# A two-layer hybrid block on one core: scale vectors as columns, squares summed by TensorE, an opening in fixed issue order, condition rows kept in DRAM

## The chip, the core and the metric

The program runs on one core of a Trainium2 chip. A core has five engines that work beside each other: TensorE (PE) for matmuls, VectorE (DVE), ScalarE (ACT), GpSimd (POOL), and SyncE (SP), which here issues the DMAs. The metric is the device time of one execution in microseconds, lower being better; shown is the median of the runs. PE weight loads appear as an engine of their own in the profile, PEld.

## What is computed

Two layers (`DEPTH` 2, `D_MODEL` 1024) over 512 latent tokens `x` and 256 context tokens `ctx`. A conditioning vector gives shift, scale and gate for the tokens, another one the same for the context. Each layer normalizes, projects once, runs four token mixers (latent attention, windowed attention, axial attention, a gated recurrence), gates and merges them, and adds the result. All is float32. The change touches only how the modulation and the normalization of layer 0 are made, and where the condition rows come from later:

```python
def _rms_norm(x, gain):
    y = x32 * lax.rsqrt(jnp.mean(x32 * x32, axis=-1, keepdims=True) + RMS_EPS)
    return (y * gain)
def _layer(x, ctx, mod_x, mod_c, lp, rope, update_ctx):
    shift_x, scale_x, gate_x = jnp.split(mod_x[:, None, :], 3, axis=-1)
    shift_c, scale_c, gate_c = jnp.split(mod_c, 3, axis=-1)
    hx = _rms_norm(x, lp['norm_w']) * (1 + scale_x) + shift_x
    hc = _rms_norm(ctx, lp['norm_w']) * (1 + scale_c) + shift_c
    px = _project_stream(hx, lp, rope, True)
    pc = _project_stream(hc, lp, None, update_ctx)
...
    sc = jax.nn.silu(c)
    scc = jax.nn.silu(c_ctx)
...
        mod_x = sc @ w_mod[l] + b_mod[l]
        mod_c = scc @ w_mod[l] + b_mod[l]
        x, ctx = _layer(x, ctx, mod_x, mod_c, lp, rope, l < DEPTH - 1)
```

## The kernel before

The streams are kept transposed: `x` and `ctx` stand as eight tiles `xk[k]` of 128 channels by 768 tokens (512 of `x`, 256 of the context). float32 matmuls of the projections are split in three: a value is kept as a rounded high half and a low half (`hi`, `lo`), and `mm3` multiplies hi·hi, lo·hi and hi·lo. So every weight tile is loaded by a DMA into `wraw`, rounded by ACT (`whi`) and subtracted by POOL (`wlo`), and every activation `hx[k]` needs its high half from ACT and its low half from a subtraction. Other matmuls, with plain float32 operands, appear as two records each.

The opening, which is what the change is about, has these steps, each with the name it has in the rows:

- `cond` (L246 and after, matmuls `scb` at L252, copies at L254): the two condition vectors, spread over all 128 partitions as rows `sc[0]` and `sc[1]` of 1024, which lie in the ring `P`. Each is made from eight matmuls 128x128 and two ACT copies. It is called for the opening, again in layer 0 in the recurrence stage, and for one row in layer 1, since attention uses `P` in between.
- `sumsq` (L286 to L290): ACT squares a tile, DVE adds it to the sum; `rstd_cols` (L299) sums over partitions on PE with two columns of ones, DVE adds epsilon (`xms`, L302) and POOL raises to the power -1/2 (L304); `rstd_rows` (L310) spreads the result as `rb`.
- `scale_pe` (L227 to L238): the scale of two channel tiles, with the two condition columns `scol` as the stationary operand and the weights moving 256 columns at a time; the result, two rows, is copied by ACT and turned into columns by two matmuls (L232), then DVE makes `mod` and `s1` (shown as `s`).
- `shift0` (L243): a shift is a DVE product-and-sum over a weight tile and a condition row, for the tokens and for the context.
- `normal` (L929): `xk` times `rb` on DVE. `hx_split` (L331 to L333): ACT writes the high half and the full value, DVE subtracts.
- `first`: the first column groups of the projection, matmuls `tk`. They accumulate tile by tile, so PE can start on `hx[0]` before `hx[1]` is there. Behind them follow matmuls `tg`, for which all eight tiles are needed, and then the head norms (`hn_ss`) and the attention.

The opening's weights come in four chunks `c`, each with two scale tiles `wmp{c}_0/1`, two shift tiles `wmp{c}_2/3` and two weight tiles for `first`. The program is written in this order, but a scheduler of the language, which works from its own timeline, sets the order of each engine's instructions; `issue_after` pins single ones. SP issues the DMAs of its queue in order, and waits there for buffers to come free.

Of the kernel before, what the change touches and what calls it, by code (L numbers as in the profile page):

```python
# [59 lines left out]
NS = len(SLOT)  # L60


def body(tc, xT, ccol, wmod, wmod0, pvec, rvec, tabs, wall, out):
# [5 lines left out]
    with st:  # L69
# [64 lines left out]
        xs = dp.tile([4, 128, 2, SEQ], F32, name="xs")  # L134

# [12 lines left out]
        def vectors():  # L148
# [72 lines left out]
        def scale_pe(c, scol, ws, p, pm):  # L221

            for q in range(2):
                w = ws[q]
                for e in range(4):
                    k = 4 * q + e
                    pe.matmul(out=p[0:2, :256], lhsT=scol[:, 2 * k:2 * k + 2], rhs=w[:, e * 256:e * 256 + 256],  # L227
                              start=(k == 0), stop=(k == 7))
            r = raw_take()
            act.activation(out=r[0:2, :256], in_=p[0:2, :256], func=AF.Copy)  # L230
            for e in range(2):
                last = pe.matmul(out=pm[:, 2 * e:2 * e + 2], lhsT=r[0:2, e * 128:e * 128 + 128], rhs=ident[0:2, 0:2],  # L232
                          start=True, stop=True, skip_group_check=True)
            f = 8 + 2 * c
            col = lambda o: pv[:, o:o + 2].unsqueeze(2).to_broadcast([128, 2, 2])
            dve.tensor_tensor(out=mod[0][:, f:f + 2, :], in0=pm[:, 0:4].rearrange("p (f i) -> p f i", f=2),
# [3 lines left out]
            return last  # L240
# [53 lines left out]

        def rstd_cols(state, n, p):
            T = n // 128
            acc = state['acc']
            for t in range(T):
                state['ins'] = pe.matmul(out=p[:, 2 * t:2 * t + 2], lhsT=acc[:, t * 128:t * 128 + 128], rhs=ones2,  # L299
                          start=True, stop=True, skip_group_check=True)  # L300
# [25 lines left out]
        def hx_split(k, i, h, xk):  # L326
# [6 lines left out]
            dve.tensor_tensor(out=h[:, 1, sl], in0=xk[:, sl], in1=h[:, 0, sl].bitcast(F32), op=ALU.subtract)  # L333
# [558 lines left out]
        scol = silu_col()  # L892
        xt = [big(f"x{kp}") for kp in range(4)]
# [4 lines left out]
        for kp in range(4):  # L898
            sp.dma_start(out=xt[kp][:, :, SEQ:], in_=xT[kp][:, :, SEQ:])
        xk = [xt[k // 2][:, k % 2, :] for k in range(KT)]  # L900
        sc = [cond(scol, i, crow[i]) for i in range(2)]
        states = [{}, {}]
        for k in range(KT):
            sumsq(xk[k][:, :SEQ], k, states[0])
# [30 lines left out]
        ms = rstd_cols(states[0], SEQ, mp[:, 384:])  # L935
        last = [scale_pe(0, scol, wm[0], mp, mp[:, 256:])]
        rstd_rows(ms, SEQ, rb)
        for c in range(4):
            for g in w0:
                w0[g].append(wload0((g, c)))  # L940
            if c < 3:
                wm.append(mod0_load(c + 1))
                with tc.issue_after(last[0].ins):
                    last[0] = scale_pe(c + 1, scol, wm[c + 1], mp, mp[:, 256:])
            ks = (2 * c, 2 * c + 1)
            for k in ks:
                shift(0, k)
            if c == 0:
                for k in range(KT):
                    normal(0, k)  # L950
            for k in ks:
                hx_split(k, 0, hx[k], xk[k])
                shift(1, k)
            for k in ks:
                first(k, (0, 2))
            if c == 0:
                for k in range(KT):
                    sumsq(xk[k][:, SEQ:], k, states[1], rawt[:, 1024:1280])
                with tc.issue_after(last[0].ins):
                    ms = rstd_cols(states[1], CTX, mp[:, 384:])  # L960
                last[0] = states[1]['ins']
                rstd_rows(ms, CTX, rb)
            for k in ks if c else ():
                normal(1, k - 2)
                hx_split(k - 2, 1, hx[k - 2], xk[k - 2])
                first(k - 2, (4,))
# [227 lines left out]
```

## Time and profile before

| | us |
|---|---|
| median of 3 runs | 1434.54 |
| lowest, highest | 1434.51, 1438.37 |
| profiled execution | 1437.18 |
| its span in the trace (2.1 lie around it) | 1435.1 |
| PE busy | 1357.7 (95%) |
| DVE, ACT, POOL busy | 895.2, 675.9, 712.3 |

Times in the rows are counted from the start of the span. A row of the timeline gives start and length of one instruction or of several alike (x4), the engine, the source line, the operation and its tiles, output before the arrow; in brackets stands how long the engine had been idle, and what ended that. Because matmuls overlap in the array, the distance of two starts is the better measure of what one costs than its own length. Lines are those of the kernel before; helpers give the same line for many tiles.

### The profile page before, as it was taken

The numbers are of one execution on the slowest core, as the hardware profiler recorded it, in microseconds if no ns is written. First come the engines' busy times: TensorE is split into PE (matmuls) and PEld (weight loads), VectorE is DVE, ScalarE is ACT, GpSimd is POOL, SyncE is SP. The second block draws the span as 40 slices with busy tenths as digits, with TensorE's granted clock in tenths as the row PEclk, the third lists the DMA queues.
The fourth block names the chain that finished last, engine by engine and source line by source line (L and its number), as shares of the span: only waits on it lengthen the run. The fifth ranks groups of instructions, "written<-read, shape, count | busy, mean of one in ns | idle before, by whom it ended". The sixth has DMA issues, their size and how long they took to land.

```text
span 1435.1 us, 21997 instructions
## 1 busy us (share of the span) xinstructions
PE 1357.7 (95%) x8216; PEld 1189.2 (83%) x8216; DVE 895.2 (62%) x1473; ACT 675.9 (47%) x1413; POOL 712.3 (50%) x691
## 2 busy tenths in 40 slices
PE   6898999999999999999999889999999999898998
PEld 4697989999998897888888778998887777776786
DVE  7756876456747656677445777876577576466441
ACT  4544555445544444562232344655555454465331
POOL 1453614223624625577553466455345563478663
PEclk8899999999999999999999999999999999999999
DMA  9301101111111212322335732112221111222544
GB/s 353 92 5 59 34 16 55 42 45 39 54 37 38 59 30 81 103 65 98 125 114 158 234 95 75 45 48 74 67 61 45 61 57 39 59 67 66 188 153 144
DMA packets 58746, 117.81 MB, mean 82 GB/s; under 512 B 6544, under 2 KB 10640, under 8 KB 58640
## 3 DMA queue, kind: packets, MB, share of 16 engines
q1 hardware_dynamic: 58640, 116.42, 25.7%
q8 instruction: 64, 1.05, 0.3%
q14 instruction: 42, 0.34, 0.1%
HBM read 112.20 MB, written 4.19 MB: 81 GB/s over the span
## 4 chain that ended last, share of the span: by engine, by line
PE 72%; DVE 9%; POOL 7%; DMA 5%; issue 4%; ACT 3%; SPq 0%; POOLq 0%; ACTq 0%; DVEq 0%
PE fg L196 9%; PE fg L195 9%; PE fg L197 9%; PE pvo L567 4%; DMA wraw<-in_wall_dram 3%; PE tg L197 3%; PE tg L196 3%; PE tg L195 3%; PE s L587 3%; POOL wlo L190 3%; PE pj L195 2%; PE pj L196 2%; PE pj L197 2%; PE ptr L560 2%; PE ptr L561 2%
## 5 line engine op out<-in xcount | busy, mean ns | idle before, releaser
L190 POOL TENSOR_TENSOR wlo<-wraw,whi 128x512 fp32r<-128x512 f32 (+2 forms) x290 | 398.8, 1378 | 360.9 <-ACT whi L189 347.3
L196 PE MATMUL fg<-hx,wlo 128*128 128x512 f32 (+1 forms) x864 | 314.2, 364 | 12.3 <-POOL wlo L190 12.3
L195 PE MATMUL fg<-hx,whi 128*128 128x512 f32 (+1 forms) x864 | 313.9, 365 | 7.9 <-ACT whi L189 5.0
L197 PE MATMUL fg<-hx,whi 128*128 128x512 f32 (+1 forms) x864 | 312.0, 361 | 0.0
L189 ACT ACTIVATE whi<-wraw 128x512 fp32r<-128x512 f32 (+2 forms) x290 | 179.8, 621 | 229.2 <-DMA wraw<-in_wall_dram 154.4
L196 PEld LDWEIGHTS fg<-hx,wlo 128*128 128x128 f32 x864 | 166.4, 193 | 38.9 <-POOL wlo L190 16.3
L195 PEld LDWEIGHTS fg<-hx,whi 128*128 128x128 f32 x864 | 165.6, 192 | 33.8 <-ACT whi L189 7.1
L197 PEld LDWEIGHTS fg<-hx,whi 128*128 128x128 f32 x864 | 166.1, 192 | 22.2
L564 DVE TENSOR_TENSOR PT<-ptr,PT 128x512 fp32r<-128x512 f32 (+1 forms) x148 | 98.5, 672 | 60.6 <-ACT PT L563 59.3
L196 PE MATMUL tg<-whi,hx 128*128 128x256 f32 (+1 forms) x432 | 122.5, 285 | 1.9 <-DVE hx L323 1.9
L195 PE MATMUL tg<-whi,hx 128*128 128x256 f32 (+1 forms) x432 | 122.2, 285 | 1.8 <-ACT hx L322 1.2
L197 PE MATMUL tg<-wlo,hx 128*128 128x256 f32 (+1 forms) x432 | 121.5, 284 | 1.4 <-POOL wlo L190 1.4
L563 ACT ACTIVATE PT<-ptr 128x512 fp32r<-128x512 f32 (+1 forms) x148 | 84.7, 585 | 79.6 <-PE ptr L561 70.0
L537 ACT ACTIVATE P<-s,nm 128x768 f32<-128x768 f32 (+3 forms) x120 | 91.9, 771 | 55.7 <-DVE nm L532 30.1
L530 DVE TENSOR_REDUCE nm<-s 128x2 f32<-128x1536 f32 (+3 forms) x60 | 86.0, 1434 | 29.5 <-PE s L197 16.9
L865 POOL TENSOR_TENSOR acc<-acc,gt 128x768 f32<-128x768 f32 (+1 forms) x48 | 81.1, 1690 | 24.1 <-DVE gt L861 23.2
L196 PEld LDWEIGHTS tg<-whi,hx 128*128 128x128 f32 x432 | 82.6, 191 | 2.8 <-DVE hx L323 2.5
L195 PEld LDWEIGHTS tg<-whi,hx 128*128 128x128 f32 x432 | 82.5, 191 | 2.8 <-ACT hx L322 1.4
L197 PEld LDWEIGHTS tg<-wlo,hx 128*128 128x128 f32 x432 | 82.4, 191 | 2.2 <-POOL wlo L190 2.0
L853 ACT ACTIVATE gt<-fg 128x512 f32<-128x512 f32 x84 | 44.1, 525 | 74.5 <-PE fg L197 70.9
L551 DVE TENSOR_SCALAR P<-P,den 128x768 f32<-128x768 f32 (+3 forms) x120 | 77.4, 685 | 1.8
L560 PE MATMUL ptr<-ident,P 128*128 128x128 f32 x288 | 72.9, 279 | 1.9 <-DVE gt L861 1.8
(302 smaller groups left out, 3137.2 us busy)
## 6 DMA issues: line engine op xcount, KB each, us to landing
wraw<-in_wall_dram SPq DMA_DIRECT2D x286, 256.0 KB, 2.6
raw<-in_wmod_dram SPq DMA_DIRECT2D x32, 512.0 KB, 3.6
wmp<-in_wmod_dram SPq DMA_DIRECT2D x16, 512.0 KB, 8.6
x<-in_xT_dram SPq DMA_DIRECT2D x4, 512.0 KB, 5.7
xs<-xn SPq DMA_DIRECT2D x4, 512.0 KB, 3.9
gt<-xs SPq DMA_DIRECT2D x8, 256.0 KB, 2.9
out_dram<-xn SPq DMA_DIRECT2D x4, 512.0 KB, 3.8
wraw<-in_wall_dram SPq DMA_DIRECT2D x8, 160.0 KB, 2.2
```

The lines of the kernel that those rows point to most:

```text
L189: act.activation(out=hi[:, :n], in_=raw, func=AF.Copy)
L190: pool.tensor_tensor(out=lo[:, :n], in0=raw, in1=hi[:, :n].bitcast(F32), op=ALU.subtract)
L195: pe.matmul(out=o, lhsT=a[0], rhs=b[0], start=first, stop=False, skip_group_check=True)
L196: pe.matmul(out=o, lhsT=a[1], rhs=b[0], start=False, stop=False, skip_group_check=True)
L197: pe.matmul(out=o, lhsT=a[0], rhs=b[1], start=False, stop=last, skip_group_check=True)
L530: dve.tensor_reduce(out=nm, in_=s3, axis=AX.X, op=ALU.max, negate=True)
L537: act.activation(out=P[i][:, :L], in_=s3[:, i, :], func=AF.Exp, scale=scale, bias=nm[:, i:i + 1], accum_out=den[:, i:i + 1])
L551: dve.tensor_scalar(out=P[i][:, :L], in0=P[i][:, :L], scalar1=den[:, i:i + 1], scalar2=None, op0=ALU.mult)
L560: pe.transpose(tr[:, e * 256:e * 256 + 128], P[0][:, ca:ca + 128], ident)
L563: act.activation(out=q[:, :n], in_=tr[:, :n], func=AF.Copy)
L564: dve.tensor_tensor(out=q[:, 512:512 + n], in0=tr[:, :n], in1=q[:, :n].bitcast(F32), op=ALU.subtract)
L865: pool.tensor_tensor(out=a[:, :N], in0=a[:, :N], in1=t[:, :N], op=ALU.add)
```

## The change

`scale_pe` takes the weights as stationary operand, 128x128 at a time, and moves the two condition columns over them, so the scale comes out as columns, without the copy and the two transposes; its DVE part becomes `scale_add`. `sumsq_pe` takes the place of `sumsq` in the opening (the later norms keep `sumsq`'s form): the square of each tile goes to PE, which sums it with the columns of ones for every 128 tokens and adds up over the eight tiles in PSUM. `hx_split` leaves the context's low half to POOL. A class `InOrder` wraps PE, ACT and DVE for the opening: each instruction is pinned behind the one before on its engine, so these three follow the written order, which is rewritten. The small vectors of the recurrence (`vectors`) are pinned on DVE behind the opening. A DRAM tile `cs` takes the two condition rows after the opening, and layers 0 and 1 read it in place of calling `cond`.

```diff
+class InOrder:
+    def __init__(self, tc, eng, last=None):
+        self.tc, self.eng, self.last = tc, eng, last
+    def __getattr__(self, name):
+        f = getattr(self.eng, name)
+        def call(*a, **k):
+            if self.last is None:
+                self.last = f(*a, **k)
+            else:
+                with self.tc.issue_after(self.last.ins):
+                    self.last = f(*a, **k)
+            return self.last
+        return call
...
+        cs = dp.tile([2, 128, 1024], F32, name="cs")
...
-        def scale_pe(c, scol, ws, p, pm):
-            for q in range(2):
-                w = ws[q]
-                for e in range(4):
-                    k = 4 * q + e
-                    pe.matmul(out=p[0:2, :256], lhsT=scol[:, 2 * k:2 * k + 2], rhs=w[:, e * 256:e * 256 + 256],
-                              start=(k == 0), stop=(k == 7))
-            r = raw_take()
-            act.activation(out=r[0:2, :256], in_=p[0:2, :256], func=AF.Copy)
-            for e in range(2):
-                last = pe.matmul(out=pm[:, 2 * e:2 * e + 2], lhsT=r[0:2, e * 128:e * 128 + 128], rhs=ident[0:2, 0:2],
-                          start=True, stop=True, skip_group_check=True)
+        def scale_pe(c, scol, ws, p):
+            for k in range(KT):
+                w = ws[k // 4]
+                for e in range(2):
+                    a = (k % 4) * 256 + e * 128
+                    pe.matmul(out=p[:, 2 * e:2 * e + 2], lhsT=w[:, a:a + 128], rhs=scol[:, 2 * k:2 * k + 2],
+                              start=(k == 0 and e == 0), stop=(k == KT - 1), skip_group_check=True)
...
+        def sumsq_pe(xk, k, sq, p):
+            n = xk.shape[1]
+            act.activation(out=sq[:, :n], in_=xk, func=AF.Square)
+            for t in range(n // 128):
+                pe.matmul(out=p[:, 2 * t:2 * t + 2], lhsT=sq[:, t * 128:t * 128 + 128], rhs=ones2,
+                          start=(k == 0 and t == 0), stop=(k == KT - 1), skip_group_check=True)
...
-            dve.tensor_tensor(out=h[:, 1, sl], in0=xk[:, sl], in1=h[:, 0, sl].bitcast(F32), op=ALU.subtract)
+            (pool if i else dve).tensor_tensor(out=h[:, 1, sl], in0=xk[:, sl], in1=h[:, 0, sl].bitcast(F32), op=ALU.subtract)
...
+        pe, act, dve = (InOrder(tc, e) for e in (nc.tensor, nc.scalar, nc.vector))
...
+        for k in range(KT):
+            sumsq_pe(xk[k][:, :SEQ], k, gt_take(), rb)
+        scale_pe(0, scol, wm[0], mp[:, 0:4])
+        ms = rstd_cols(None, SEQ, rb)
+        scale_add(0, mp[:, 0:4])
         rstd_rows(ms, SEQ, rb)
...
             ks = (2 * c, 2 * c + 1)
+            if c == 0:
+                for k in ks:
+                    normal(0, k)
             for k in ks:
                 shift(0, k)
+                hx_split(k, 0, hx[k], xk[k])
+            first(ks[0], (0, 2))
+            q = mp[:, 4 * c + 4:4 * c + 8]
+            if c < 3:
+                scale_pe(c + 1, scol, wm[c + 1], q)
+            first(ks[1], (0, 2))
             if c == 0:
+                for k in range(2, KT):
+                    normal(0, k)
+            if c < 3:
+                scale_add(c + 1, q)
+            if c == 1:
                 for k in range(KT):
...
+                    sumsq_pe(xk[k][:, SEQ:], k, gt_take(), rb)
+                rstd_rows(rstd_cols(None, CTX, rb), CTX, rb)
+                for k in range(4):
+                    shift(1, k)
+                for k in range(KT):
+                    normal(1, k)
+            if c == 2:
+                for k in ks:
+                    shift(1, k)
+                for k in (0, 1):
+                    context(k)
         for k in (6, 7):
...
+            shift(1, k)
+        for k in range(2, KT):
+            context(k)
+        boot = dve.last
+        pe, act, dve = nc.tensor, nc.scalar, nc.vector
         consts()
+        for i in range(2):
+            sp.dma_start(out=cs[i], in_=sc[i])
...
-                sc = [cond(scol, i, crow[i]) for i in range(2)]
+                for i in range(2):
+                    sp.dma_start(out=sc[i], in_=cs[i])
...
-                sc = [cond(scol, 0, crow[0])]
+                sp.dma_start(out=sc[0], in_=cs[0])
```

On PE, from the start to the first `tk`, the kernel before has this order (`ones_92` are the columns of ones, `scol` the condition columns, `P` in the second row the sum of squares):

```order
L252 MATMUL scb<-ident,scol 128x128 x16
L299 MATMUL mp<-ones_92,P 128x2 x4
L227 MATMUL mp<-wmp_0_123,scol 2x256 x4
L227 MATMUL mp<-wmp_1_124,scol 2x256 x4
L310 MATMUL rb<-ident,xms 128x128 x4
L232 MATMUL mp<-ident,raw 128x2 x2
```

In the changed kernel all rows of the opening have a line of `InOrder`, and PE has there:

```order
L73 MATMUL scb<-ident,scol 128x128
L76 MATMUL scb<-ident,scol 128x128 x15
L76 MATMUL rb<-ones_92,gt 128x2 x32
L76 MATMUL mp<-scol,wmp_0_124 128x2 x8
L76 MATMUL mp<-scol,wmp_1_125 128x2 x8
L76 MATMUL rb<-ident,xms 128x128 x4
```

The four sums over partitions have become 32, the eight scale matmuls 16 with two columns, and the transposes are gone.

On DVE, between the normals of the tokens and the low halves of tiles 0 to 3, before has among others this piece (`ISA raw,mod_99` with the row under it is one shift):

```order
L236 TENSOR_TENSOR mod_99<-mp,consts 128x4
L333 TENSOR_TENSOR hx_0_175<-x_115,hx_0_175 128x512
L333 TENSOR_TENSOR hx_1_176<-x_115,hx_1_176 128x512
L243 ISA raw,mod_99<-wmp_3_351,P,consts 128x1024
L243 ISA mod_99 128x1
L243 ISA wmp_2_350,mod_99<-wmp_2_350,P,consts 128x1024
L243 ISA mod_99 128x1
L290 TENSOR_TENSOR raw<-raw,gt 128x256
```

For the same two tiles the changed kernel has:

```order
L76 ISA raw,mod_99<-wmp_2_126,P,consts 128x1024
L76 ISA mod_99 128x1
L76 TENSOR_TENSOR hx_0_157<-x_116,hx_0_157 128x512
L76 ISA raw,mod_99<-wmp_3_127,P,consts 128x1024
L76 ISA mod_99 128x1
L76 TENSOR_TENSOR hx_1_158<-x_116,hx_1_158 128x512
```

A shift now stands directly ahead of the low half of its own tile, where before the shifts of a chunk stood well ahead of its low halves, with other chunks' shifts and adds between.

On SP, around the layer-0 recurrence, the two reloads of the condition rows (into `P`) stand behind the recurrence's own weights and ahead of the next weight tiles:

```order
L795 DMA wraw<-in_wall_dram 128x512 x2
L1086 DMA P<-cs 128x1024 x2
L208 DMA wraw<-in_wall_dram 128x512 x3
L281 DMA raw<-in_wmod_dram 128x1024
L208 DMA wraw<-in_wall_dram 128x512 x2
```

Before, there was no DMA between the first two rows on `wraw`. Outside the opening and the two recurrence stages the order of all engines is nearly the same in both kernels.

## Rows read from the trace of the kernel before

**Rows 1.** Timeline of the opening to 22 us: start, us, engine, line, operation [idle].

```profile
3.31 6.69 PE L252 MATMUL scb<-ident,scol 128*128 128x128 f32 x32 [3.31 <-DVE scol L209]
...
9.99 3.08 DVE L290 TENSOR_TENSOR P<-P,gt 128x512 f32<-128x512 f32 x4 [1.01 <-ACT gt L289]
...
10.86 1.14 ACT L289 ACTIVATE gt<-x 128x512 f32<-128x512 f32 x2
11.91 0.58 ACT L254 ACTIVATE P<-scb 128x512 f32<-128x512 f32 x1
...
13.13 1.87 PE L299 MATMUL mp<-ones,P 128*128 128x2 f32 x8 [3.13 <-DVE P L290]
...
15.28 2.06 POOL L304 TENSOR_TENSOR xms<-xms,mhalf 128x4 f32<-128x4 f32 x1 [14.00 <-DVE xms L302]
...
20.93 1.16 PE L310 MATMUL rb<-ident,xms 128*128 128x128 f32 x8
```

**Rows 2.** Timeline, 22 to 59 us: normals, scale, shift, `hx` and the first `tk`.

```profile
22.70 3.07 DVE L929 TENSOR_TENSOR x<-x,rb 128x512 f32<-128x512 f32 x5
...
25.90 5.30 PE L227 MATMUL mp<-wmp,scol 128*2 128x256 f32 x16 [3.29 <-DVE mod L236]
...
29.16 1.28 DVE L243 CUSTOM_DVE_ANT_0 raw<-wmp,P,consts 128x1024 bf16<-128x1024 f32 x1
...
31.52 1.50 ACT L332 ACTIVATE x<-x,mod,s 128x512 f32<-128x512 f32 x2
...
34.73 1.29 DVE L333 TENSOR_TENSOR hx<-x,hx 128x512 fp32r<-128x512 f32 x2
...
35.47 0.39 PE L196 MATMUL tk<-w,hx 128*128 128x256 f32 x1 [3.07 <-DVE hx L333]
...
56.00 2.73 DVE L929 TENSOR_TENSOR x<-x,rb 128x256 f32<-128x256 f32 x8
```

**Rows 3.** Timeline, DVE and POOL from 42 us.

```profile
42.41 4.00 POOL L190 TENSOR_TENSOR w<-wraw,w 128x512 fp32r<-128x512 f32 x2 [17.69 <-ACT w L189]
...
42.97 2.30 DVE L243 CUSTOM_DVE_ANT_0 wmp<-wmp,P,consts 128x1024 f32<-128x1024 f32 x1
```

**Rows 4.** Timeline, end of the opening: last low halves, first `tg`, end of `tg`.

```profile
77.19 2.12 DVE L333 TENSOR_TENSOR hx<-x,hx 128x512 fp32r<-128x512 f32 x4 [3.36 <-ACT x L332]
...
88.80 0.28 PE L195 MATMUL tg<-whi,hx 128*128 128x256 f32 x1
...
106.08 0.39 PE L195 MATMUL fg<-hx,whi 128*128 128x512 f32 x1
```

**Rows 5.** Instructions of line 299: records, ns min/median/max, first and last start.

```profile
L299 PEld LDWEIGHTS mp<-ones,P x8: 288/334/338, 13.1 to 14.6; 128*128 128x128 f32 x8
...
L299 PE MATMUL ssp<-ones,P x8: 165/252/252, 827.1 to 827.8; 128*128 128x2 f32 x8
```

**Rows 6.** Busy us by stretch: length, PE, PEld, DVE, ACT, POOL, clock, DMA, GB/s.

```profile
13.00:14.00 1.00, 0.87 (x4) 0.87 (x5) 0.08 (x1) 0.00 (x0) 0.00 (x0) 0.50 1.04 400
20.00:21.00 1.00, 1.00 (x6) 0.30 (x4) 1.00 (x3) 0.12 (x1) 0.80 (x1) 1.00 1.00 393
20.00:30.00 10.00, 6.71 (x29) 3.04 (x28) 9.89 (x18) 2.90 (x7) 3.05 (x2) 0.83 1.04 398
100.00:110.00 10.00, 8.45 (x63) 7.80 (x62) 7.02 (x19) 3.87 (x11) 9.25 (x13) 1.00 0.09 26
110.00:120.00 10.00, 8.01 (x52) 6.77 (x50) 7.64 (x13) 3.74 (x9) 7.08 (x8) 1.00 0.27 80
120.00:130.00 10.00, 8.34 (x34) 6.67 (x35) 6.64 (x14) 4.79 (x13) 2.05 (x2) 0.83 0.16 52
```

**Rows 7.** Chain that ended last, in the two recurrence stages: start, us, what.

```profile
548.99 0.89 PE scb L252 x8
...
556.95 2.76 DMA wraw<-in_wall_dram
...
1327.14 2.70 DMA wraw<-in_wall_dram
```

More of the change, by code (lines that the diff above doesn't have):

```diff
@@ L146, in consts, with vectors @@
             dve.tensor_copy(out=maskb, in_=mask)
-        def vectors():
+        def vectors(last):
+            dve = InOrder(tc, nc.vector, last)
             ab = tp.tile([128, 8], F32, name="sp_ab", tag="sm")
@@ L239, in scale_pe @@
                                      in1=col(PV_NORM + 2 * c), op0=ALU.add, op1=ALU.mult)
-            return last
         def shift0(f, i, sc, w, out):
@@ L293, in rstd_bcast @@
             return rstd_rows(rstd_cols(state, n, tps("ssp")), n, tps("rb"))
+        def sumsq_pe(xk, k, sq, p):
[4 more added lines that the diff above has]
+                          start=(k == 0 and t == 0), stop=(k == KT - 1), skip_group_check=True)
         def rstd_cols(state, n, p):
             T = n // 128
-            acc = state['acc']
-            for t in range(T):
-                state['ins'] = pe.matmul(out=p[:, 2 * t:2 * t + 2], lhsT=acc[:, t * 128:t * 128 + 128], rhs=ones2,
+            for t in range(T) if state else ():
+                pe.matmul(out=p[:, 2 * t:2 * t + 2], lhsT=state['acc'][:, t * 128:t * 128 + 128], rhs=ones2,
                           start=True, stop=True, skip_group_check=True)
@@ L933, in shift, with context @@
             shift0(k, i, sc[i], w, w if i else rawt[:, 1536:2048].bitcast(BF16))
-        ms = rstd_cols(states[0], SEQ, mp[:, 384:])
-        last = [scale_pe(0, scol, wm[0], mp, mp[:, 256:])]
+        def context(k):
+            hx_split(k, 1, hx[k], xk[k])
+            first(k, (4,))
+        for k in range(KT):
[3 more added lines that the diff above has]
+        scale_add(0, mp[:, 0:4])
         rstd_rows(ms, SEQ, rb)
@@ L940, in body @@
                 w0[g].append(wload0((g, c)))
+            if c == 1:
+                for kp in range(4):
+                    sp.dma_start(out=xt[kp][:, :, SEQ:], in_=xT[kp][:, :, SEQ:])
             if c < 3:
                 wm.append(mod0_load(c + 1))
-                with tc.issue_after(last[0].ins):
-                    last[0] = scale_pe(c + 1, scol, wm[c + 1], mp, mp[:, 256:])
             ks = (2 * c, 2 * c + 1)
+            if c == 0:
+                for k in ks:
+                    normal(0, k)
@@ L946, in body @@
             for k in ks:
                 shift(0, k)
-            if c == 0:
-                for k in range(KT):
[L950 to L956, printed above, removed]
-                for k in range(KT):
[L958 to L966, printed above, removed]
-        for k in (6, 7):
-            normal(1, k)
-            hx_split(k, 1, hx[k], xk[k])
-            first(k, (4,))
+                hx_split(k, 0, hx[k], xk[k])
[4 more added lines that the diff above has]
+            first(ks[1], (0, 2))
@@ L1024, in body @@
             if l == 0:
-                with tc.issue_after(wdma[0].ins):
-                    vectors()
+                vectors(boot)
             m1 = branch(SWA)
```

9 lines of the change are left out of this document (3 added, 6 removed).

## The prediction, made before the changed kernel was run

> **What bounds the kernel now.** The chip runs the program for 1437.18 us in the profiled execution; TensorE is busy nearly everywhere outside the opening, so I read first where it is not. The table by stretches [rows 6] shows TensorE about two thirds busy from 20 to 30 us with VectorE at 9.89 of 10, and losses again from 100 to 130 us. I then went through the timeline of the opening, engine by engine. Up to 22 us it is one chain [rows 1]: condition copies on TensorE and ScalarE, squares on ScalarE, adds on VectorE (the last end at 13.07), a two-column sum on TensorE, the scale run, the power on GpSimd (ends 17.34), the row broadcast, which ends at 22.09. From there VectorE holds the pace: normals, shifts and the low halves of `hx` follow without a gap, and TensorE waits 3.07 us for the first low half [rows 2]. The last low half ends at 79.31, the last `tk` matmul of the opening starts shortly before 88.8, and the 144 `tg` matmuls that follow run to 106.08 [rows 4]; that is 17.3 us, or 0.12 each, which is also the price of a `tk` matmul at full clock. I use 106.1 as the clock of the opening: the instruction order behind it is almost the same in both kernels, so what the opening gains or loses by then is carried to the end unless the stalls behind it absorb it.
>
> **Up to the row broadcast.** The order of ScalarE changes: the four copies of the condition rows stand ahead of all squares. TensorE ends its 32 `scb` records at 10.00 and a copy takes 0.58 [rows 1], so the copies end near 10.7, the first square near 11.3, and TensorE begins on it near 11.4; before, the last square had ended at 12.0. Before, ScalarE's squares were hidden under TensorE's condition matmuls; that cover is gone. The seven adds leave VectorE. In their place TensorE has 32 matmuls of 128x2, which by the pairs in the trace (four instructions, eight records) are 64 records, and the scale is 16 such matmuls, 32 records, in place of the run of 16 records by 5.30 us, with the ScalarE copy and the transposes also gone [rows 2].
>
> The price of such a record is the first open term. It was 0.213 us at 13.1 us (eight in 1.87 with the last one's tail) at granted clock 0.50, that is 1.2 GHz, and half of that, 0.107, at 827 us [rows 5, 6]; I call the two half and full clock. At full clock from the start: ScalarE feeds squares by 0.57 each, TensorE takes 8x0.107 = 0.86 for each, so the squares end at 11.4+6.9 = 18.3, the scale at 21.7 and the broadcast at 22.6 (its power of 2.06 runs beside the scale): +0.5 against 22.1. At half clock throughout: 11.4+13.6+6.8+1.7 = 33.5: +11.4. I take the middle from the same place: before, TensorE began at 13.13 at half clock, and the row of 20 us has full clock [rows 6]. So the first half of the squares goes at 0.213, to 18.2, the other half in 3.4, the scale in 3.4, the broadcast in 0.9: 25.9. **+3.8**, between +0.5 and +11.4.
>
> The Trainium skill states in "TensorE: Matmul & The Clock Gate", section "LDWEIGHTS (loading the stationary operand)", that the load of a stationary takes its columns divided by 1.2 in nanoseconds, by which 128 columns are an estimated 107 ns whatever the clock, and 64 squares 6.8 us. The rows at 13.1 us disagree: the same records are 0.213 apart there, and loads themselves 0.334 long. By the rule this term would be +0.5; it stands below as a rival by the full-clock price, which rows give too.
>
> **From the broadcast to the last low half.** The order is now fixed by hand: VectorE has shift k, then low half k, with nothing between, while ScalarE makes `hx` and `x` from that shift. Before, other shifts and normals always stood between. So per k the time is serial: 1.3 for a shift with its readout, two ScalarE passes of 0.75, a low half of 0.65 and some 0.15 of hand-overs: 3.6, for eight 28.7 [rows 2]. To that come 8 normals by 0.61 = 4.9, 8 of the context by 0.34 = 2.7, the six context shifts ahead of the last `hx` low half by 1.3 = 7.9, and small additions and the like, 1.3. Sum 45.5. VectorE also waits in this order for TensorE four times: for scale 1, scale 2, the context's sum of squares and scale 3, each queued behind 24 `tk` matmuls that need the low half just made (24x0.12 = 2.9 us). At full clock the waits are 0 to 2.4, 2.7, 6.3 and 2.7: 11.7; with two-column records at half clock 24.3. VectorE's next shift, low half and, through ScalarE's own fixed order, everything behind are queued behind each wait. Full clock gives 57.2, which happens to be exactly the 57.2 of before (79.3 less 22.1): the gain of fewer adds is paid back by stalls. Of the three scale runs behind the first one in the trace, I have two near half clock (such as the 5.30 one) and one faster, so I take half of the way: 18.0, together 63.5. **+6.3**, between 0 and +12.6.
>
> One row speaks for more: a shift that fell on a GpSimd subtraction took 2.30 in place of 1.28 [rows 2, 3]. The Trainium skill has this in "SBUF — State Buffer", section "Who interferes with whom": a VectorE instruction with two SBUF inputs and a GpSimd one that reads SBUF exclude each other. It speaks against the part of the change that moves eight context subtractions to GpSimd: each collision would cost up to 1.0 by that row. I leave it out of the sum, as the collisions existed before.
>
> **From the last low half to the end of `tg`.** Left for TensorE then: 24 `tk` of tile 7, six context tiles of 12 matmuls, 144 `tg`: 2.9+8.6+17.3 = 28.8, against 106.1-79.3 = 26.8: **+2.0**. The end of `tg` so moves by 3.8+6.3+2.0 = 12.1, to 118.2.
>
> **What stands behind it.** From 100 to 130 us TensorE is idle for 5.2 us, and about 1.7 more go to the lower clock from 120 to 130 [rows 6]: there the head norms on VectorE and GpSimd are late. In the new order the tokens' `tk` end 25.9 before the end of `tg` rather than about 22, so these norms start some 3.8 earlier; but GpSimd has six context subtractions of about 0.7, 4.2, in the same stretch, and VectorE the 25 small vector steps. I set **0**, from -6.9 (all loss recovered) to +4.2.
>
> **Condition rows.** Saving them is 1 MB on SP's queue ahead of the second pair of weights, some 2.7 us of transfer by the pace of the opening; those weights are needed only at k = 2, over ten us later, and are there. With a later opening that cover only grows. In layer 0, the reload replaces 32 records of 0.111, four times 0.89 on the path: **-3.6** [rows 7]. The reload is queued ahead of the `wraw` of 556.95. Its buffers, which the condition's copies write today, are free by 549.9 at the latest, when the last `scb` record ends, so two transfers of about 1.3 by the opening's pace end well before 556.95; were they late, they would delay these weights by at most 2.7. In layer 1 the 16 records lie where weights come late (the `wraw` transfer of 1327.14 ends the wait), so I set 0, at most -0.6.
>
> **Sum.** 12.1+0-3.6 = +8.5 on 1437.2, that is 1445.7 for a profiled execution; the median of the runs before is 1434.54, so **1443.0** for the median.
>
> **Rivals.** *Full clock in the opening, no change* (0.26): two-column records keep TensorE at 2.4 GHz or load at one price at either clock. Then 0.5+0+2.0-3.6 = -1.1: 1433.4. For it: 827 us, and that TensorE now waits little before the squares. Against: full clock there came after dense work, and half clock at 13.1 with the same instruction. *Full clock and the stalls behind close, faster* (0.21): the mechanism is the earlier start of the head norms, at 100 to 130 us; if GpSimd has room, TensorE finds its operands and gets back up to 6.9, giving 1433.4-6.9 = 1426.5, or 1429.6 with only the 3.8 of the earlier start. It decides from 3.2 us recovered, given full clock. For it: the idle rows of GpSimd in 120 to 130; against: 9.25 of 10 busy in 100 to 110. *Half clock throughout* (0.12): 11.4+12.6+2.0-3.6 = +22.4: 1456.9. *The forecast* (0.41), from about +4.5 to +16. That the opening does not do what it says is no rival of weight: the order is fixed in the code.
>
> **How the numbers follow.** About 0.3%, 4.3 us, is what a measurement of this kernel can tell from no change, so faster lies under 1430.2 and slower over 1438.8. The two slow cases make 0.53 slower; the same case gives 0.25; faster is 0.22, nearly all of the closing case and a little of a full clock that loses less at the scale waits. The range leaves out the far half of the half-clock case and the far part of the faster one: 1428 to 1453.
>
> **What would show it.** Squares: 64 records from about 11.4, at 0.213 apart and granted clock 0.50 for the first half, and the broadcast's end near 26; if it is at 22 to 23, the first term is the rival's. VectorE idle about 1.6 before each low half of `hx`, on ScalarE's `x`; if it is less, the per-k time was too long. The four waits of VectorE on TensorE, 18 in all. `tg` ending near 118.2. Four fewer groups of `scb` near 545 and no new wait at 557. I am wrong as a whole if the stretch from the end of `tg` to 136 us shrinks by more than 5, or if VectorE's order lets more overlap than I see.

## The result

The changed kernel is slower: 1461.32 us median of four runs (1458.74 to 1462.0) against 1434.58, a ratio of 1.0177 with an interval of 1.0156 to 1.0197. I had forecast slower, at 1443.0 within 1428 to 1453; the loss is three times the 8.5 us that I had summed, and the time lies outside the range.

The profiled execution took 1461.56, its span is 24.7 us longer than before. The page of the changed kernel, its engines and the granted clock in 40 slices of 36.5 us:

```profile
PE 1375.4 (94%) x8300; PEld 1219.6 (84%) x8300; DVE 888.9 (61%) x1451; ACT 671.1 (46%) x1403; POOL 712.3 (49%) x699
...
PEclk6679999999999999999999999999999999999999
```

DVE has less to do, as intended (888.9 against 895.2 us), but the clock of the first three slices is at 0.6 to 0.7, where before it stood at 0.8, 0.8 and 0.9 or more. PE has 17.7 us more busy time with 8300 records in place of 8216: where the clock is at half, the same records take longer.

The timeline of PE, from the squares to the first `tk` (start, us, engine, line, operation, in brackets the idle time and its cause), and the table by stretches for the same time (columns as in [rows 6]):

```profile
10.28 10.38 PE L76 MATMUL rb<-ones,gt 128*128 128x2 f32 x64 [1.20 <-ACT gt L76]
20.52 6.97 PE L76 MATMUL mp<-scol,wmp 128*128 128x2 f32 x32
27.34 2.05 PE L76 MATMUL rb<-ident,xms 128*128 128x128 f32 x8
32.90 0.58 PE L76 MATMUL tk<-w,hx 128*128 128x256 f32 x1 [3.50 <-ACT hx L76]
```

```profile
10.00:14.00 4.00, 3.73 (x34) 3.73 (x34) 0.00 (x0) 3.15 (x6) 0.00 (x0) 1.00 1.02 365
14.00:20.00 6.00, 6.00 (x31) 6.00 (x30) 0.29 (x1) 2.30 (x4) 2.51 (x2) 0.51 1.04 407
20.00:27.00 7.00, 7.00 (x35) 7.00 (x34) 0.16 (x1) 0.00 (x0) 1.03 (x1) 0.50 1.04 388
```

PE works from 10.3 on without a gap. The granted clock is full at first (2.4 GHz, a record every 0.112 us) and falls to half (1.2 GHz, 0.213) at 14 us in the middle of the squares. The scale then takes 6.97 for 32 records, 0.213 each, and the broadcast ends at 29.39 against 22.09 before [rows 1].

From there DVE and PE take turns. DVE in the changed kernel; the rows are its four waits for PE, with the last low half of `hx`:

```profile
43.42 0.16 DVE L76 TENSOR_TENSOR mod<-mp,consts 128x4 f32<-128x4 f32 x1 [1.79 <-PE mp L76]
...
54.92 0.16 DVE L76 TENSOR_TENSOR mod<-mp,consts 128x4 f32<-128x4 f32 x1 [3.88 <-PE mp L76]
...
63.68 0.16 DVE L76 TENSOR_SCALAR xms<-rb 128x2 f32<-128x2 f32 x1 [8.40 <-PE rb L76]
...
88.05 0.16 DVE L76 TENSOR_TENSOR mod<-mp,consts 128x4 f32<-128x4 f32 x1 [8.36 <-PE mp L76]
...
100.16 0.69 DVE L76 TENSOR_TENSOR hx<-x,hx 128x512 fp32r<-128x512 f32 x1 [1.81 <-ACT x L76]
```

The other half of the turn is PE's: from 64 to 75 us it is busy for 1.68 of 11, while DVE works through shifts and normals. The last low half ends at 100.85 (79.31 before, [rows 4]), and `tg` at 129.73 (106.08 before): the opening is 23.6 us longer. Of the 24.7 us of the span that is nearly all.

What is left lies in two stages behind. The first transposes of the attention come 21.0 later than before (165.1 against 144.1) and so does the first matmul of the layer-0 recurrence (547.5 against 526.5); the first output matmul of layer 0 comes 24.1 later (796.7 against 772.6). So 2.6 us are won back in the head norms, and 3.1 are lost in the recurrence stage, where I had counted on winning 3.6.

### The profile page after: what moved, and what is told of

Same layout as the page of the kernel before. It is cut to its first block, busy times and chain, and to the rows that moved or that the text cites. A ratio compares the mean times of both kernels' runs of the same rounds, so it can differ in the third digit from the quotient of the medians.

```text
span 1459.8 us, 22150 instructions
## 1 busy us (share of the span) xinstructions
PE 1375.4 (94%) x8300; PEld 1219.6 (84%) x8300; DVE 888.9 (61%) x1451; ACT 671.1 (46%) x1403; POOL 712.3 (49%) x699
## 5 line engine op out<-in xcount | busy, mean ns | idle before, releaser
L210 POOL TENSOR_TENSOR wlo<-wraw,whi 128x512 fp32r<-128x512 f32 (+2 forms) x290 | 394.5, 1363 | 369.0 <-ACT whi L209 345.0
```

The source lines that it names most:

```text
L210: pool.tensor_tensor(out=lo[:, :n], in0=raw, in1=hi[:, :n].bitcast(F32), op=ALU.subtract)
```

## The experiments

Three causes are to be told apart: the fixed order (its turns between DVE and PE), the half clock under two-column matmuls, and the stored rows. The expectations call the first theory O and the second theory C. The table has one profiled execution of each; times at marks are us from the start of its span. The ratio is that of the timed runs to the kernel before on the same chip, with its interval. Executions of one kernel differ by up to 10 us, as the runs of before show (1432 to 1442), and the profiled ones of e2, e4, e9 and e14 took 4 to 8 us longer than their kernels' medians; so the marks say where, the ratios how much. The median of before itself was 1434.6 to 1438.6 in the sets of runs that the ratios refer to. In before, e4 and e15 the last low half on DVE is one of the context, 0.7 to 1.8 us behind the last one of the tokens.

| kernel | broadcast starts | last low half ends | `tg` ends | median | ratio |
|---|---|---|---|---|---|
| before | 20.9 | 79.3 | 106.1 | 1434.6 | 1 |
| changed | 27.3 | 100.9 | 129.7 | 1461.3 | 1.0177 (1.0156 to 1.0197) |
| e1: wide columns | 21.6 | 93.6 | 123.3 | 1460.3 | 1.0151 (1.0122 to 1.0180) |
| e2: shifts ahead | 30.3 | 100.0 | 134.1 | 1462.2 | 1.0178 (1.0139 to 1.0217) |
| e3: old sums and scale, fixed order | 21.2 | 104.1 | 133.6 | 1474.3 | 1.0257 (1.0221 to 1.0292) |
| e4: before with stored rows | 21.4 | 80.9 | 106.6 | 1436.7 | 0.9986 (0.9962 to 1.0009) |
| e8: no fixed order | 30.6 | 79.9 | 110.0 | 1435.1 | 0.9991 (0.9971 to 1.0010) |
| e9: another fixed order | 30.5 | 93.6 | 125.0 | 1460.7 | 1.0150 (1.0113 to 1.0187) |
| e10: e9 with wide columns | 21.1 | 75.3 | 106.7 | 1439.1 | 1.0017 (0.9997 to 1.0038) |
| e11: e8 with wide columns | 23.5 | 68.4 | 94.7 | 1433.5 | 0.9961 (0.9939 to 0.9983) |
| e12: e11 with condition matmuls | 23.7 | 74.4 | 99.1 | 1435.4 | 0.9975 (0.9953 to 0.9997) |
| e13: order on PE and ACT only | 30.4 | 88.3 | 121.1 | 1452.0 | 1.0107 (1.0078 to 1.0136) |
| e14: order on ACT and DVE only | 32.8 | 94.3 | 123.9 | 1451.5 | 1.0092 (1.0059 to 1.0124) |
| e15: e11 with context halves on DVE | 23.6 | 69.5 | 94.8 | 1432.2 | 0.9967 (0.9952 to 0.9982) |

A mark in the opening is not yet a time of the kernel. From the end of `tg` to the first transposes of the attention the fourteen traces take 31.5 to 42.4 us, with no clear relation to the opening: e4, whose opening is that of before, has the 42.4, and before itself 38.0.

**e1: 128 columns in place of two.** The edit to the changed kernel (the scale likewise, with the pair of condition columns repeated 64 times):

```diff
-                pe.matmul(out=p[:, 2 * t:2 * t + 2], lhsT=sq[:, t * 128:t * 128 + 128], rhs=ones2,
...
+                pe.matmul(out=p[:, 128 * t:128 * t + 128], lhsT=sq[:, t * 128:t * 128 + 128],
+                          rhs=ones2[:, 0:1].to_broadcast([128, 128]),
...
```

> The changed kernel, but the matmuls of the squares and of the scale move 128 columns (the ones, or the condition column pair repeated 64 times) over the same stationary operands, in place of two. Number of matmuls, weight loads and order are the same. Theory C (the two-column matmuls leave TensorE at half clock, and that is most of the loss): no fall of the granted clock at 14 us, squares 0.111 apart, row broadcast done near 23 in place of 29.4, VectorE's four waits on TensorE about 12 us together in place of 22.4, tg ends near 110 (129.7 in the changed kernel), median 1437 to 1444. Theory O (the fixed order with its serial steps is the loss, and the clock falls because TensorE waits): the clock falls at about the same place, tg ends at 125 to 130, median 1456 to 1462.

PE's timeline of e1, the same 64 and 32 records:

```profile
10.81 7.41 PE L76 MATMUL rb<-ones,gt 128*128 128x128 f32 x64 [1.21 <-ACT gt L76]
18.06 3.73 PE L76 MATMUL mp<-scol,wmp 128*128 128x128 f32 x32
```

The work is larger and the time smaller: a record every 0.113, and the clock column stays at 1.00 through the squares. So up to the broadcast the half clock of the changed kernel comes from the narrow matmuls, with PE equally without gaps in both. The broadcast is done at 22.7, about as before. But the rest of theory C fell: the last low half still ends at 93.6 and `tg` at 123.3. From the broadcast to the last low half 70.9 us pass, against 71.5 in the changed kernel, although the mean granted clock in this stretch is 0.79 against 0.65 (before: 0.88). DVE in e1 shows why; the waits remain, and some lengths have grown:

```profile
36.85 1.28 DVE L76 SCALAR_TENSOR_TENSOR s<-mod,consts 128x4 f32<-128x4 f32 x1
38.06 2.38 DVE L76 CUSTOM_DVE_ANT_0 raw<-wmp,P,consts 128x1024 bf16<-128x1024 f32 x1
...
57.47 0.16 DVE L76 TENSOR_SCALAR xms<-rb 128x2 f32<-128x2 f32 x1 [6.15 <-PE rb L76]
...
88.74 1.16 DVE L76 TENSOR_TENSOR hx<-x,hx 128x512 fp32r<-128x512 f32 x1 [5.27 <-ACT x L76]
```

The first two rows run beside two POOL subtractions (36.82 to 39.36): 0.16 has become 1.28, and 1.28 has become 2.38. The last one waits for ACT, which stands at that place behind roundings of weights that have not landed. The median gains 1 us only: of the 6.4 by which `tg` ends earlier, 3.4 are left at the first matmul of the recurrence (544.1 against 547.5) and 1.1 at the first output matmul (795.6 against 796.7).

**e3: the order alone.** Both PE parts are undone, `sumsq` on DVE and the old scale; the order stays fixed.

```diff
-            sumsq_pe(xk[k][:, :SEQ], k, gt_take(), rb)
+            sumsq(xk[k][:, :SEQ], k, states[0])
...
-        scale_pe(0, scol, wm[0], mp[:, 0:4])
+        r = scale_pe(0, scol, wm[0], mp)
...
             first(ks[1], (0, 2))
+            if c < 3:
+                scale_cols(r, q)
```

> The changed kernel with both TensorE parts undone: squares added by VectorE, one sum over partitions by four matmuls, scale with the condition columns stationary and 256 weight columns moving, ScalarE copy and two transposes (behind the next 24 tk matmuls). The fixed order, the context subtraction on GpSimd and the stored condition rows stay. Theory C: granted clock mostly full from 20 us on, row broadcast near 24, tg ends near 110 to 114, median 1438 to 1446. Theory O: the serial order still costs, tg ends at 122 to 130, median 1453 to 1462.

It is the slowest of all: the two-column matmuls are refuted as the main cause. In the fixed order DVE here waits 25.7 us for the scale of PE in four waits, the longest 8.67, and the seven context adds stand in the same chain. The clock is not full here either: from the broadcast to the last low half its mean is 0.71 (e4, with nearly the same operations in the scheduler's order: 0.88), and PE is busy for 49.4 of 80.8 us. So half clock comes with this order even without the narrow matmuls, and is part of its price. The new PE parts are worth some 11 us in this order (1.0257 to 1.0177); it is the order that costs.

**e2: both shifts of a chunk ahead.**

```diff
             for k in ks:
                 shift(0, k)
+            for k in ks:
                 hx_split(k, 0, hx[k], xk[k])
```

> The changed kernel, but in each chunk both shifts of VectorE stand ahead of the two tiles' high and low halves, so that the second shift covers ScalarE's two passes. Theory O: each of the four pairs saves 1.3 to 1.7 us on the path, 5 to 7 us, median 1454 to 1456. Theory C: VectorE is ahead of TensorE at the four waits anyway, so what it gains there is waited out, except before the first tk and after the last wait: 1 to 3 us, median 1458 to 1460.

From the end of the broadcast (32.3) to the last low half 67.7 us pass, against 71.5 in the changed kernel, so 3.7 are saved there, between the two expectations. DVE's waits for ACT on the low halves fall from 14.2 to 5.0, its four waits for PE grow from 22.4 to 25.8, and collisions with POOL from 3.4 to 5.3: a part of what is gained ahead of a wait is waited out in it. The total does not change; in this execution, 8 us above the median, the squares also lost full clock earlier, at 12.4 us (12.59 for the 64).

**e8: the order taken out.**

```diff
-        pe, act, dve = (InOrder(tc, e) for e in (nc.tensor, nc.scalar, nc.vector))
...
-                vectors(boot)
+                with tc.issue_after(wdma[0].ins):
+                    vectors()
```

> The changed kernel without the fixed order: the class that pins each instruction of TensorE, ScalarE and VectorE behind the one before is taken out, so the scheduler orders the opening again, as in the kernel before. The columns, the squares on TensorE, the context subtraction on GpSimd and the stored rows stay. After the first four runs there are two causes: the fixed order makes VectorE and TensorE wait for each other in turn (some 17 us of the 23.6 by which tg ends late, as the run with wide columns has it), and the two-column matmuls' half clock (some 6). Theory O: without the order tg ends at 108 to 116, median 1436 to 1447. Theory C: half clock remains with its full price, tg ends at 120 to 130, median 1452 to 1462.

The whole loss is gone, 0.9991, with the two-column matmuls in place. They are as slow as in the changed kernel, and the broadcast is done later still, at 32.65. From e8's timeline:

```profile
30.60 2.05 PE L332 MATMUL rb<-ident,xms 128*128 128x128 f32 x8
32.96 6.99 PE L246 MATMUL mp<-scol,wmp 128*128 128x2 f32 x32 [0.31 <-DVE mod L252]
```

```profile
30.00:40.00 10.00, 9.69 (x45) 9.39 (x46) 9.96 (x19) 3.91 (x6) 1.57 (x1) 1.00 0.98 385
```

The scheduler puts the second chunk's scale there, where in the fixed order PE waits for the first `hx`; PE idles for 0.3 us between 10 and 100 us. (The clock column says 1.00 here, though 32 records take 6.99, the pace of half clock: ahead of the first change of clock that this trace has on record the column tells nothing, and the pace has to.) The edit also lets the small vectors of the recurrence go again, as in before. In the changed kernel they start at 103.66, behind the last low half, so they are not what made the opening late up to there.

**e13 and e14: on which engine.** One engine at a time is left to the scheduler; e13 also lets the small vectors go, as e8 does. The notes at the end of the lines name the run.

```diff
-        pe, act, dve = (InOrder(tc, e) for e in (nc.tensor, nc.scalar, nc.vector))
+        pe, act = (InOrder(tc, e) for e in (nc.tensor, nc.scalar))     # e13
+        act, dve = (InOrder(tc, e) for e in (nc.scalar, nc.vector))    # e14
```

> The changed kernel with the fixed order kept on TensorE and ScalarE, and VectorE left to the scheduler. If the loss sits in VectorE's order (shift and low half in turn, the scale additions ahead of the next shifts): tg ends at 112 to 120, median 1440 to 1450. If it sits in TensorE's (scale between two tiles' tk, nothing to fill the waits): tg ends at 122 to 130, median 1453 to 1462.

> The mirror of the run before: the fixed order kept on ScalarE and VectorE, TensorE left to the scheduler, which puts the second chunk's scale ahead of the row broadcast. If TensorE's order is the cause: tg ends at 108 to 116, median 1436 to 1446. If VectorE's is: tg ends at 118 to 128, median 1450 to 1460.

Each gives back somewhat less than half (1.0107 and 1.0092). e13 ends between its two expectations, e14 where VectorE's order was to be the cause. Neither of the two orders carries the loss alone. ACT's order was fixed in both runs, and no run frees or fixes it alone, so its own share is not known. With PE's order fixed, DVE still waits 9.0 for the scale and 7.7 for the context's sum; with DVE's fixed, DVE waits 15.6 for ACT on the low halves and 11.3 for the context's sum, and PE stands idle from 70 to 80 us for 5.8 of 10.

**e9 and e10: a better order, then both.** On DVE the next chunk's shifts stand in the gaps, the scale additions behind them, and the context's sum is read a chunk later. The core of it:

```diff
+        fill = {0: ([lambda: shift(0, 1)], [lambda: normal(0, 2), lambda: normal(0, 3)]),
+                1: ([lambda: shift(0, 4)], [lambda: shift(0, 5)]),
...
-            for k in ks:
-                shift(0, k)
+                shift(0, 0)
+            for k, fs in zip(ks, fill[c]):
+                for f in fs:
+                    f()
                 hx_split(k, 0, hx[k], xk[k])
...
+            if c == 2:
+                ms = rstd_cols(None, CTX, rb)
+                rstd_rows(ms, CTX, rb)
+                for k in range(KT):
+                    normal(1, k)
```

> The changed kernel with another fixed order: on VectorE the next chunk's shifts and the normals stand ahead of the low halves and of the scale additions, so that they run while ScalarE makes the halves and while TensorE has the 24+32+24 matmuls; the context's sum of squares is read one chunk later. Same instructions on every engine. Theory O (not that an order is fixed, but that this one makes the two engines take turns): VectorE's waits fall from some 36 to under 20, tg ends 10 to 16 earlier than in the changed kernel, at 114 to 120, median 1445 to 1451. Rival (TensorE at half clock is the longer side anyway): tg ends at 123 to 128, median 1455 to 1460.

> The other order of the run before in this list, with 128 columns moving in the squares and the scale. If order and clock are both causes and add up: tg ends 5 to 8 earlier than with two columns, at 107 to 114, median 1437 to 1445. If the order alone counts: within 2 of the run with two columns.

The order alone moves the end of `tg` by 4.7, the columns alone (e1) by 6.4; both together by 23.0, to 106.7, as before the change. So they don't add up. A part of that is chance: in e9 the squares lost full clock at 12.2 us, not at 14.1, and its broadcast ends 3.1 later than in the changed kernel. From the end of the broadcast to the last low half the changed kernel takes 71.5, e1 70.9, e9 61.1 and e10 53.1, and in it, behind the first normal, DVE waits for PE 22.4, 16.4, 13.2 and 8.4 us. So wide columns save 0.5 in the old order and 8.0 in the new one; that each cause holds back the gain of the other is how I read these waits, no run shows it by itself. e9's PE, then DVE in e9 and in e10 at the same place, the normals of the context behind the broadcast:

```profile
10.99 12.78 PE L76 MATMUL rb<-ones,gt 128*128 128x2 f32 x64 [1.20 <-ACT gt L76]
23.63 6.97 PE L76 MATMUL mp<-scol,wmp 128*128 128x2 f32 x32
```

```profile
84.35 2.73 DVE L76 TENSOR_TENSOR x<-x,rb 128x256 f32<-128x256 f32 x8 [9.97 <-PE rb L76]
```

```profile
66.03 2.73 DVE L76 TENSOR_TENSOR x<-x,rb 128x256 f32<-128x256 f32 x8 [6.73 <-PE rb L76]
```

By the ratios, which rest on several executions each, the two together give back 0.016 of 0.0177, where each alone gives 0.003.

**e11, e12, e15: no fixed order and wide columns.** e11 is e8 with the edit of e1. e12 has `cond` again in place of the reloads (shown for layer 0, likewise in layer 1; the saving is gone), e15 the context's subtraction on DVE:

```diff
-                for i in range(2):
-                    sp.dma_start(out=sc[i], in_=cs[i])
+                sc = [cond(scol, i, crow[i]) for i in range(2)]
```

```diff
-            (pool if i else dve).tensor_tensor(out=h[:, 1, sl], in0=xk[:, sl], in1=h[:, 0, sl].bitcast(F32), op=ALU.subtract)
+            dve.tensor_tensor(out=h[:, 1, sl], in0=xk[:, sl], in1=h[:, 0, sl].bitcast(F32), op=ALU.subtract)
```

> Without the fixed order and with 128 columns moving in the squares and the scale. If the two causes are all there is, this is the kernel before again or better in the opening: tg ends at 100 to 108, median 1428 to 1438. If something else in the change costs (the context subtraction on GpSimd, the vectors of the recurrence moved behind the opening), tg still ends over 112.

> The run without fixed order and with wide columns, and in it the condition rows made again by the condition matmuls, as before, in place of stored rows. The run with the stored rows alone on the kernel before gave no clear difference. If the reload gains what the prediction had (3.6): 3 to 4 us slower than the same run with stored rows, ratio to before about 0.999. If the matmuls only filled waiting time: within 1.5 us of it, ratio 0.995 to 0.998.

> The run without fixed order and with wide columns, with the context's low halves on VectorE again. If the move to GpSimd costs (collisions of the two engines, and later head norms): 1 to 3 us faster than that run, ratio 0.994 to 0.995. If it helps, since VectorE is the engine without idle time from 30 to 60 us: 1 to 3 us slower.

e11 beats both kernels, if by little: 0.9961. Its opening is 11.4 us shorter than that of before, and of that 2.2 arrive in the span of these two traces, 2.5 in the medians, 5.6 by the ratio. The stages behind give it back: from the end of `tg` to the first transposes of the attention e11 needs 41.1 us (94.7 to 135.8), before 38.0 (106.1 to 144.1), which is within what this stage varies; at the first matmul of the recurrence 6.2 are left (520.3 against 526.5), at the first output matmul 2.4. PE's longest wait in the first of these stages, in e11:

```profile
98.28 0.80 PE L215 MATMUL fg<-hx,wlo 128*128 128x512 f32 x1 [3.23 <-POOL wlo L209]
```

POOL is busy with head norms at that moment (9.41 of 10 from 90 to 100 us), and the weights' low half stands behind them, as in [rows 6] at 100 us. Whether the context's subtraction is on POOL or DVE makes no difference that these runs can tell (0.9961 and 0.9967).

**e4: the stored rows alone.** The edit of layer 0; layer 1 likewise, and the saving behind the opening.

```diff
-                sc = [cond(scol, i, crow[i]) for i in range(2)]
+                for i in range(2):
+                    sp.dma_start(out=sc[i], in_=cs[i])
```

> The kernel before with one part of the change alone: the two condition rows are saved in DRAM behind the opening and read back in layers 0 and 1 in place of the condition matmuls. As the prediction had it: the 32 records of layer 0 were on the path, -3.6, median 1430.5 to 1431.5. Rival: they filled time in which TensorE would have waited for the recurrence's VectorE and GpSimd steps, so their removal opens waits and lowers the clock: median 1434 to 1438.

The median is 2.0 lower than before's on that chip (1438.6), with an interval that includes 1. e12 against e11 is as weak: 0.9975 and 0.9961, 2 us in favour of the stored rows, intervals overlapping. In the stage itself the gain is not to be seen. From the first matmul of the recurrence to the first output matmul, before takes 246.1 us and e12, the other one with condition matmuls, 244.4; the twelve traces with stored rows take 246.0 to 251.5. PE in the changed kernel at that place, and the table for the ten us:

```profile
567.89 0.33 PE L583 MATMUL ptr<-ident,P 128*128 128x128 f32 x1 [1.16 <-DVE P L574]
569.76 0.33 PE L584 MATMUL ptr<-ident,P 128*128 128x128 f32 x1 [1.55 <-DVE P L574]
```

```profile
567.00:577.00 10.00, 7.56 (x29) 6.09 (x30) 4.42 (x6) 1.69 (x4) 5.04 (x4) 0.83 0.30 105
```

Before has the condition matmuls there, and this row:

```profile
546.00:556.00 10.00, 10.00 (x73) 9.34 (x73) 2.76 (x7) 5.39 (x11) 5.46 (x5) 1.00 0.01 2
```

So the 32 records were a filling: without them PE waits for DVE's scaling of `P`, which in turn took 2.47 for two instructions beside a POOL addition, and is at half clock for the matmuls behind. The idle time of PE bears it out: from the first matmul of the recurrence to the first output matmul it is 8.2 us in before and 9.1 in e12, and 12.0 to 14.3 in the twelve traces with stored rows. The removed 3.6 us of matmuls come back as idle time. The chain of waits had them on it [rows 7], which was true and did not mean that the path behind would move up.

## Why the prediction was wrong, step by step

*Up to the broadcast: +3.8 forecast, +7.3 measured*, within the bounds (+0.5 to +11.4). The half and half came out the other way round: PE had begun the squares at full clock and lost it at 14 us. In the other three traces with the same run of 64 records (e2, e9, e13) the fall comes at 12.2 to 12.9 us and the broadcast ends at 32.3 to 32.5, up to +10.4, so the term is nearer to its upper bound than one trace tells. I had taken the course of the kernel before, from half to full; there PE had two-column matmuls for 1.87 us only, and then the scale with 256 columns moving.

The Trainium skill's rule that I weighed there, in "TensorE: Matmul & The Clock Gate", section "LDWEIGHTS (loading the stationary operand)", divides the columns by 1.2 and has no clock in it, an estimated 107 ns for 128 columns. The trace does not agree: in the squares, loads of 128 columns took 0.19 us at full and 0.33 at half clock, and the records were 0.112 and 0.213 apart. So the single figure does not hold, and the rival that goes by one price at either clock fell with it.

*From the broadcast to the last low half: 63.5 forecast (57.2 to 69.8), 71.5 measured, above the upper bound.* This is the first of two steps that failed, and the larger one. Its mechanism was right, in each part: per tile 3.6 (measured 3.63, from one low half to the next), and four waits for PE. What failed is the size of two terms. First, the waits: I took half of the way between the clocks, 18.0, and they measured 22.4, near the half-clock figure of 24.3. The broadcast's term had the same open question; the two were one uncertainty, and I treated them as two that would even out. Second, I put collisions of DVE with POOL at nothing, "as the collisions existed before". In the changed kernel these four run beside POOL subtractions:

```profile
63.76 2.41 DVE L76 CUSTOM_DVE_ANT_0 wmp<-wmp,P,consts 128x1024 f32<-128x1024 f32 x1
...
88.24 0.95 DVE L76 SCALAR_TENSOR_TENSOR s<-mod,consts 128x4 f32<-128x4 f32 x1
...
94.92 1.18 DVE L76 TENSOR_TENSOR hx<-x,hx 128x512 fp32r<-128x512 f32 x1 [2.11 <-ACT x L76]
96.03 2.31 DVE L76 CUSTOM_DVE_ANT_0 raw<-wmp,P,consts 128x1024 bf16<-128x1024 f32 x1
```

They took 2.41, 0.95, 1.18 and 2.31 where 1.28, 0.16, 0.69 and 1.28 are due, 3.4 together, and in a chain without slack each one counts. The 4.4 of the waits and these 3.4 are nearly all of the 8.0 by which the term was short; what is left of the 71.5, 45.6, agrees with the 45.5 that I had summed for the work.

The price at full clock was too low as well, and e1 shows by how much at least in part: 70.9 (22.7 to 93.6, at a mean clock of 0.79) where I had 57.2. Of the 13.7 the waits for PE are 4.7 (16.4 against 11.7), six collisions 5.4, and ACT's late tile 6 3.5 (5.27 against the usual 1.73). That figure of 57.2, the same as before's, carried the rivals "no change" and "faster" with 0.47 of the chance; e1 is the nearest to their case, full clock up to the broadcast, and it took 1460.3.

*From the last low half to the end of `tg`: 28.8 forecast, 28.9 measured.* PE works without a gap from 100.91 on, as forecast.

*Behind: 0 forecast, -2.6 measured*, within the bounds. It is no sign that the stage takes up a part of the loss: it varies from 31.5 to 42.4 over the traces, and in e3, with a loss as large, it is 1.2 longer than before.

*Stored rows: -3.6 forecast, +3.1 measured in that stage.* This is the second step that failed, and here the mechanism was wrong: the 32 records were taken to be on the path. The DMAs were hidden, as said, though each took 3.1 to 3.3 us and not 1.3: the second landed at 573.5, and the next weights were issued at 580.3. The saving was not one. The prediction asked of each transfer what hides it, and did not ask of the removed matmuls what they hid.

The sum of what was measured: 7.3+14.3+2.1-2.6+3.1 = 24.2 of 24.7, where 3.8+6.3+2.0+0-3.6 = 8.5 was forecast. Of the 16.2 between them the broadcast has 3.5, the stretch behind it 8.0 and the stored rows 6.7; the head norms take 2.6 off.

*The rivals.* "Half clock throughout" had 0.12 and came to 1456.9; with the stored rows' 3.6 not won it would have been within a microsecond of the result. That is luck in part: its first term, 11.4, measured 7.3, and a longer stretch up to the last low half and the 3.1 lost in the recurrence stage made up for most of it. Its weight was too small because the one row that spoke for full clock (827 us) had eight records in it, and the change issues 224.

What stays open: why the clock falls at 14.1 us in one execution and at 12.2 in another (10.38 and 12.78 for the same 64 records), what share of the loss ACT's fixed order has, what makes the stages behind the opening vary, and the gain or loss of the stored rows over the whole kernel, which is smaller than what these runs tell.

## What to carry to other kernels

When an order is written by hand for engines that feed each other, give every wait something to stand behind it: put the next stage's independent work ahead of an instruction that waits for another engine, and count each wait at the slowest pace that engine may have. Before removing work from a busy engine, look at what the others do meanwhile; work that fills a wait is free, and its removal shows the wait. Read a gain at the end of the kernel, not at a mark: of 11.4 us won in e11's opening, 2.2 to 5.6 arrived. And where two terms of a sum hang on the same unknown, they are high together.

## What the runs showed of the hardware

Granted clock did not follow PE's being busy. In the changed kernel PE is busy for 6.00 of 6 us from 14 on, at a clock of 0.51, and for 7.00 of 7 from 20 on, at 0.50. With 64 matmul records back to back, those that move two columns began at full clock and lost it on the way, in four traces of four (changed, e2, e9, e13: 10.38 to 12.78 us, the fall at 12.2 to 14.1). The same loads with 128 columns moving kept it (e1 and e10: 7.41 us). Moving more made it faster. In this kernel's opening that was worth 18.3 us in one order (e9 to e10, 125.0 to 106.7) and 6.4 in another (changed to e1).

DVE instructions that fell on a POOL subtraction took longer: 1.28 where 0.16 is usual, and 2.38 where 1.28 is (e1). The four of the changed kernel cost 3.4 us, the six of e1 5.4.
